# A nine-stage network on one core: scheduled layer boundaries and a first squared-relu MLP with 512-token products

## The chip, the cores and the metric

The kernel runs on one core of one Trainium2 chip. The metric is the time of one execution on the device, in microseconds (us), without the transfer of inputs and outputs to and from the host. The engines of the core are TensorE (PE, with its weight loads PEld beside it), VectorE (DVE), ScalarE (ACT), GpSimd (POOL) and SyncE (SP), which here only issues transfers. L12 in a row means line 12 of the kernel that the row was taken from.

## The reference

One sequence of 512 tokens, width 1024, runs through two networks. The first has a mixer of two attentions, a cross attention to 256 memory rows and a SwiGLU MLP of width 2816. The second has two layers: an mLSTM and an MLP, then an attention with compressed keys and values (MLA) and an MLP. All of it is float32. Every part takes a normalised stream and adds its normalised output to it; in the second network shift, scale and gate come from a conditioning vector:

```python
ada = cond @ ada_w[l] + ada_b[l]
sh1, sc1, g1, sh2, sc2, g2 = jnp.split(ada, 6, axis=-1)
h = modulate(rmsnorm(x, norm_g[l, 0]), sh1, sc1)
...
x = x + g1[:, None, :] * rmsnorm(y, norm_g[l, 1])
h = modulate(rmsnorm(x, norm_g[l, 2]), sh2, sc2)
y = sqrelu_mlp(h, mlp_w1[l], mlp_w2[l])
x = x + g2[:, None, :] * rmsnorm(y, norm_g[l, 3])
```

with `sqrelu_mlp(h, w1, w2) = jnp.square(jax.nn.relu(h @ w1)) @ w2`, inner width 4096, and `modulate(h, shift, scale) = h * (1 + scale) + shift`.

## The kernel before

**Products.** Every float32 operand is split into a high part (a rounded copy, made by ACT) and a low part (the rest, made by DVE), and a product of two operands is three matmuls: high by high, high by low, low by high (L447, L448, L449 in `prod`). Weights come by DMA from SP's queue into `raw` tiles and are split there: L307 and L308 plain, L317 and L318 with a gain in it. Activations are split by `parts` (L626 on ACT, L627 on DVE). The stream `x` stays in four tiles of 128 tokens; what a product reads is its normalised, transposed and split form `h`, an `HT` (tiles of all 512 tokens) or an `HS` (quarters of 256 tokens by four blocks of rows).

**The two squared-relu MLPs** (`relu2`, `mlp`) take their 32 hidden tiles in blocks of 6, 8, 6, 6 and 6, and add each block's down product to a sum in SBUF. Where `h` is an `HS`, which is so in both, blocks 1 to 4 go by `wino`: a pair of hidden tiles is made by seven products of 256 tokens in place of eight (L510). `split7` makes the seven weight combinations (subtractions and additions L342, L345, L361 on DVE, splits L341 on ACT), `quarters` the seven of the activations (with POOL's L482), and the results are put together from PSUM by copies on ACT and additions on DVE (L520 to L534). Block 0, and every product of an `HT`, goes by `relu_pairs`: plain products of two weight columns tiles of 128 at a time.

**Layer boundaries** (`boundary`, L634). The last block's down product of each stage yields its rows by token tile. For each of the four token tiles `a` adds the sum to `x` and takes the mean of squares (L579 on ACT, L568 and L562 on POOL), `scaled` normalises it (L598 on ACT, two halves of 512 columns), and `put` transposes it on PE (L608), modulates it where the next part wants that (two of four columns on DVE L616, two on ACT L619, into a new tile), and splits it (L626, L627), half after half. `first` is the next stage's first product, which yields at each point the token tiles it needs. All this ran in `self.ordered()`: on PE, ACT, DVE and POOL the instructions stood in the order in which the code names them. Outside, a list scheduler orders the program by priority and a model of times.

**Background.** The rows of `ada` are made by a generator that `step` calls once for each 2.0 us of PE work (`pace`, `pacb`): weights by DMA (L868, POOL's queue), multiplied on DVE (L863), summed over rows by one matmul (L881), written to `arow` in DRAM, and fetched as columns by `cols_steps` (L381 to L388: a DMA, three yields, a transpose on PE at L386).

## Time and profile before

| what | us |
|---|---|
| median of three runs | 2026.44 |
| lowest, highest | 2026.16, 2029.08 |
| profiled execution | 2028.55 |
| its span | 2026.5 |

The span is from the first to the last instruction of the profiled execution; 2.05 us lie around it. The stages follow each other in the span so: mixer 0 to 476, cross attention to 545, SwiGLU to about 833, mLSTM to about 1045, first squared-relu MLP 1075 to 1457, attention to about 1650, second squared-relu MLP from 1667 to 2019. Neighbours overlap by some microseconds, since a stage's first products run beside the boundary of the one before. PE's busy time is that of matmul instructions with modelled ends; a time in which PE waits is named by the instruction that waited and by the one whose end released it.

### The profile page before, as it was taken

What the parts mean: (1) busy time and instruction counts of PE and PEld (TensorE: products, weight loads), DVE (VectorE), ACT (ScalarE), POOL (GpSimd) and SP (SyncE); (2) the same over time, 40 slices, a digit from 0 to 9 for tenths busy, and PEclk for the clock granted to TensorE, in tenths of its full rate; (3) what the DMA queues carried; (4) which work ended last, traced back from release to release, by engine and by line L of the source; (5) the groups of instructions that cost most, each with busy time, mean ns of one, the idle gap of its engine ahead of it and who ended that gap; (6) DMA issues with size and microseconds to landing.
All of it is one profiled execution on the core that took longest, in us unless ns stands there. A gap on an engine that the chain in (4) does not pass through costs nothing. (4 is left out here: it accounts for less than half of the span.)

```text
span 2026.5 us, 29742 instructions
## 1 busy us (share of the span) xinstructions
PE 1943.2 (96%) x10738; PEld 1663.4 (82%) x10738; DVE 1373.4 (68%) x2689; ACT 1073.1 (53%) x2355; POOL 355.6 (18%) x711
## 2 busy tenths in 40 slices
PE   7999999999999999899999899998889989999997
PEld 5888988878888888678888788888687879989996
DVE  5756655856666665576866888898568747657665
ACT  6767775545353243556446464455465556545543
POOL 1331111201122211121323221222120012000000
PEclk9999999999999999999999999999999999999999
DMA  6322342523465554153442354565243212233321
GB/s 198 89 79 65 113 136 74 187 73 115 136 208 177 161 172 116 52 169 101 154 135 84 110 162 138 185 188 165 62 114 94 84 63 73 73 114 105 104 85 62
DMA packets 175251, 242.01 MB, mean 119 GB/s; under 512 B 20108, under 2 KB 117537, under 8 KB 175105
## 3 DMA queue, kind: packets, MB, share of 16 engines
q1 hardware_dynamic: 150704, 170.53, 27.2%
q0 software_dynamic: 24400, 69.60, 11.5%
q8 instruction: 84, 1.38, 0.3%
q14 instruction: 63, 0.51, 0.1%
HBM read 237.88 MB, written 2.20 MB: 118 GB/s over the span
## 5 line engine op out<-in xcount | busy, mean ns | idle before, releaser
L447 PE MATMUL ps<-s,s 128*128 128x512 f32 (+4 forms) x2276 | 863.0, 381 | 26.7 <-ACT s L626 25.1
L448 PE MATMUL ps<-s,s 128*128 128x512 f32 (+4 forms) x2276 | 851.6, 375 | 2.8 <-DVE s L627 1.9
L449 PE MATMUL ps<-s,s 128*128 128x512 f32 (+4 forms) x2276 | 849.7, 375 | 1.5 <-DVE s L627 1.4
L447 PEld LDWEIGHTS ps<-s,s 128*128 128x128 f32 (+2 forms) x2276 | 432.0, 190 | 105.9 <-ACT s L626 31.0
L449 PEld LDWEIGHTS ps<-s,s 128*128 128x128 f32 (+2 forms) x2276 | 431.2, 190 | 83.2 <-DVE s L627 5.2
L448 PEld LDWEIGHTS ps<-s,s 128*128 128x128 f32 (+2 forms) x2276 | 432.3, 190 | 79.1 <-DVE s L627 4.0
L510 PEld LDWEIGHTS ps<-s,s 128*128 128x128 f32 x2184 | 261.8, 188 | 6.7 <-DVE u L526 4.5
L510 PE MATMUL ps<-s,s 128*128 128x256 f32 x2184 | 263.7, 281 | 3.6 <-DVE u L526 3.6
L307 ACT ACTIVATE s<-raw 128x512 fp32r<-128x512 f32 x277 | 157.8, 622 | 143.2 <-PE ps L449 97.9
L308 DVE TENSOR_TENSOR s<-raw,s 128x512 fp32r<-128x512 f32 x277 | 190.3, 726 | 57.0 <-ACT s L307 55.7
L863 DVE SCALAR_TENSOR_TENSOR u<-araw,cond,u 128x512 f32<-128x512 f32 x224 | 167.3, 747 | 24.2 <-DMA araw<-in_ada_w 15.4
L317 ACT ACTIVATE s<-raw,cols_all 128x256 fp32r<-128x256 f32 (+1 forms) x305 | 143.5, 546 | 66.5 <-PE ps L449 29.8
L318 DVE SCALAR_TENSOR_TENSOR s<-raw,cols_all,s 128x256 fp32r<-128x256 f32 (+1 forms) x305 | 147.6, 538 | 39.3 <-ACT s L317 38.7
L868 POOL DMA_DIRECT2D araw<-in_ada_w x192 | 104.0, 542 | 338.0 <-DVE u L863 289.2
L627 DVE TENSOR_TENSOR s<-u,s 128x512 fp32r<-128x512 f32 x126 | 87.0, 700 | 79.4 <-ACT s L626 56.7
L626 ACT ACTIVATE s<-u 128x512 fp32r<-128x512 f32 x126 | 77.6, 625 | 63.8 <-PE ps L449 31.9
L568 POOL TENSOR_SCALAR sm<-sm,sm 128x1 f32<-128x1 f32 x34 | 10.5, 307 | 527.5 <-ACT junk L579 527.4
L341 ACT ACTIVATE s<-raw 128x512 fp32r<-128x512 f32 x104 | 62.7, 621 | 72.7 <-PE ps L449 37.6
L627 DVE TENSOR_TENSOR s<-ps,s 128x512 fp32r<-128x512 f32 (+3 forms) x100 | 59.1, 606 | 42.4 <-ACT s L626 35.0
L341 ACT ACTIVATE s<-u 128x512 fp32r<-128x512 f32 x78 | 48.7, 624 | 66.8 <-DVE u L345 36.4
L342 DVE TENSOR_TENSOR s<-raw,s 128x512 fp32r<-128x512 f32 x104 | 70.7, 683 | 15.4 <-ACT s L341 15.1
L1358 DVE TENSOR_TENSOR u<-ps,u 128x512 f32<-128x512 f32 x80 | 53.9, 685 | 34.3 <-PE ps L449 33.6
(261 smaller groups left out, 2162.9 us busy)
## 6 DMA issues: line engine op xcount, KB each, us to landing
raw<-in_mlp_w SPq DMA_DIRECT2D x128, 512.0 KB, 3.8
araw<-in_ada_w POOLq DMA_DIRECT2D x192, 256.0 KB, 3.5
raw<-in_w_gate_up SPq DMA_DIRECT2D x44, 512.0 KB, 4.1
raw<-in_w_in SPq DMA_DIRECT2D x24, 512.0 KB, 4.2
raw<-in_a_w_in SPq DMA_DIRECT2D x24, 512.0 KB, 3.8
raw<-in_w_down SPq DMA_DIRECT2D x22, 512.0 KB, 3.7
raw<-in_w_mem_kv SPq DMA_DIRECT2D x16, 512.0 KB, 3.6
araw<-in_kv_ada_w POOLq DMA_DIRECT2D x32, 256.0 KB, 4.0
```

The lines of the kernel that those rows point to most:

```text
L307: A.activation(hi[:, sl, cl], src[:, sl, cl], AF.Copy)
L308: f.tensor_tensor(out=lo[:, sl, cl], in0=src[:, sl, cl], in1=hi[:, sl, cl].bitcast(F32), op=ALU.subtract)
L317: A.activation(hi[:, i, :], src[:, i, :], AF.Copy, scale=g)
L318: V.scalar_tensor_tensor(out=lo[:, i, :], in0=src[:, i, :], scalar=g, in1=hi[:, i, :].bitcast(F32), op0=ALU.mult, op1=ALU.subtract)
L341: A.activation(hi, x, AF.Copy)
L447: self.nc.tensor.matmul(ps, lhsT=ah, rhs=bh, start=first and i == 0, stop=False)
L448: self.nc.tensor.matmul(ps, lhsT=ah, rhs=bl, start=False, stop=False)
L449: self.nc.tensor.matmul(ps, lhsT=al, rhs=bh, start=False, stop=last and i == n - 1)
L510: nc.tensor.matmul(ps, lhsT=l[:, k, :], rhs=m[:, k, :], start=first and k == e == 0, stop=k == 3 and e == 2, skip_group_check=True)
L627: self.nc.vector.tensor_tensor(out=lo, in0=x, in1=hi.bitcast(F32), op=ALU.subtract)
L863: V.scalar_tensor_tensor(out=acc, in0=raws.pop(j), scalar=vec[:, j:j + 1], in1=acc, op0=ALU.mult, op1=ALU.add)
L868: nc.gpsimd.dma_start(out=raws[j], in_=ws[:, j, :])
```

## The change

Five things change.

1. The first squared-relu MLP gets its activations as an `HT`. So `relu2` takes all its blocks by `relu_pairs`, 512 tokens at a time, and neither `wino`, `split7` nor `quarters` is called there. The second keeps its `HS`.
2. `boundary` no longer runs in `self.ordered()`; no layer boundary has a fixed order. The boundary's own steps get a higher priority (`self.hot("hb")`, an offset of 300). With `fixed=False`, which only the first squared-relu MLP's boundary has, they also stand in another place of the program: `put` of the tile two before and all `scaled` ahead of the next stage's first products.
3. `put` modulates both halves of a token tile, in place in the normalised tile, and then splits both.
4. `pace` and `pacb` go from 2.0 to 1.9, `lc` (weight tiles split ahead in an MLP's last block) from 7 to 6, and `cols_steps` yields five times between its DMA and its transpose.
5. At the start the tiles 1 to 3 of `x` are fetched two or so weight tiles earlier.

```diff
-        for _ in range(3):
+        for _ in range(5):
             yield None
...
+        todo = []
         for y, cw in ys:
...
-            hi, lo = h.blk(k, n, tt(t))
             if mod:
                 g, sh = mod
-                y = self.u2((P, n, P))
+                y = y.rearrange("p (n c) -> p n c", c=P)
...
                 ps = y
+            todo.append((k, n, ps))
+            k += n
+        for k, n, ps in todo:
+            hi, lo = h.blk(k, n, tt(t))
             self.parts(hi, lo, ps)
-            k += n
...
-        with self.ordered():
+        hot = lambda: self.hot("hb")
+        with nullcontext():
...
-                    if n == 4 and nxt and t >= 2:
+                    if n == 4 and nxt and t >= 2 and fixed:
                         self.put(*pend.pop(t - 2))
-                if nxt and t >= 1:
-                    scaled(t - 1)
-                rs[t] = a(t, ys, ss)
+                with hot():
+                    if nxt and t >= 2 and not fixed:
+                        self.put(*pend.pop(t - 2))
+                    if nxt and t >= 1:
+                        scaled(t - 1)
+                    rs[t] = a(t, ys, ss)
             if nxt:
-                i = -1
+                if not fixed:
+                    with hot():
+                        scaled(NT - 1)
                 for i, need in enumerate(first):
-                    if i == late[0]:
+                    if fixed and i == late[0]:
                         scaled(NT - 1)
-                    for n, t in ((1, NT - 2), (2, NT - 1)):
-                        if i == late[n]:
-                            self.put(*pend.pop(t))
+                    for t in sorted(pend):
+                        if t <= need if not fixed else i >= late[t - 1]:
+                            with hot():
+                                self.put(*pend.pop(t))
...
-        self.before = {2: [lambda: get(1)], 4: [lambda: get(2), lambda: get(3)], 6: [biases]}
+        self.before = {1: [lambda: get(1)], 3: [lambda: get(2), lambda: get(3)], 6: [biases]}
...
-        hn = HS(self, KD)
+        hn = HT(self, KD)
         self.out_lin(a["a_w_out_2"][0], ho, g, nxt(4, 3, hn), self.relu_pairs(hn, a["mlp_w1_2"][0], 0, BUF["fp"], True), "head")
```

Lines behind the changed ones shift by up to ten: L881 and L598 of before are L891 and L598 of after, L626 is L629, L1693 is L1703.

The order on PE just behind the boundary before the first squared-relu MLP, before: L881 sums a background row, L386 transposes columns, and the others are products; the numbers behind a name tell tiles apart.

```order
4853 L448 MATMUL ps_10803<-s_2021_10571,s_1989_10414 128x256
4854 L449 MATMUL ps_10803<-s_2021_10571,s_1989_10414 128x256
4855 L881 MATMUL ps_10855<-u_2052_10828,onesr_78 128x512
4856 L386 MATMUL ps_10911<-ident_66,u_2055_10873 128x8
4857 L447 MATMUL ps_10979<-s_1995_10449,s_2044_10785 128x512
```

The same place in the changed kernel:

```order
4875 L449 MATMUL ps_11018<-s_2062_10814,s_2097_11010 128x512
4876 L891 MATMUL ps_11103<-u_2106_11082,onesr_78 128x512
4877 L447 MATMUL ps_11018<-s_2062_10814,s_2097_11010 128x512
...
4930 L449 MATMUL ps_11134<-s_2066_10876,s_2081_10914 128x512
4931 L386 MATMUL ps_11187<-ident_66,u_2111_11125 128x8
4932 L447 MATMUL ps_11134<-s_2066_10876,s_2080_10913 128x512
```

The transpose stood directly behind the row's sum; now 54 product matmuls stand between the two.

The order on PE where the last block's down product of the first squared-relu MLP begins, before. L510 are the seven products of the last pairs, s_2453, s_2454 and s_2498 the hidden tiles: one to four in the first two, five and six in the last.

```order
5622 L447 MATMUL ps_14007<-s_2489_13903,s_2453_13669 128x512
5623 L448 MATMUL ps_14007<-s_2489_13903,s_2453_13669 128x512
5624 L510 MATMUL ps_13831<-s_2021_10571,s_2473_13795 128x256 x12
5625 L449 MATMUL ps_14007<-s_2489_13903,s_2454_13670 128x512
5626 L510 MATMUL ps_13833<-s_2064_10938,s_2474_13814 128x256 x12
5627 L447 MATMUL ps_14007<-s_2493_13942,s_2498_13975 128x512
```

The same place in the changed kernel; ps_13109 is the last hidden tile's product, s_2386 and s_2387 hold hidden tiles one to four and s_2404 five and six.

```order
6072 L449 MATMUL ps_13109<-s_2017_10495,s_2382_13015 128x512
6073 L447 MATMUL ps_13197<-s_2390_13072,s_2386_13027 128x512
...
6084 L449 MATMUL ps_13197<-s_2392_13091,s_2387_13028 128x512
6085 L447 MATMUL ps_13197<-s_2398_13146,s_2404_13177 128x512
...
6088 L447 MATMUL ps_13222<-s_2400_13165,s_2386_13027 128x512
...
6101 L448 MATMUL ps_13222<-s_2407_13190,s_2404_13177 128x512
6102 L447 MATMUL ps_13197<-s_2398_13146,s_2404_13177 128x512
```

Before, a product with the fifth hidden tile stood right behind the last of the seven products. Now the 15 rows from 6073 to 6087 and the 14 from 6088 to 6101 use hidden tiles one to five, and row 6102 is the first with the sixth.

The order on ACT at the boundary behind that MLP, before: L579 takes mean squares, of x or of a tile u of the attention, L598 normalises, L317 splits weights.

```order
1132 L579 ACTIVATE junk_14319,sm_14318<-x_11_92 128x1024
1133 L317 ACTIVATE s_2562_14261<-raw_13994,cols_2283_12462 128x384
1134 L317 ACTIVATE s_2568_14279<-raw_14003,cols_2283_12462 128x384 x2
1135 L317 ACTIVATE s_2569_14288<-raw_14264,cols_2283_12462 128x384
1136 L579 ACTIVATE junk_14371,sm_14370<-u_2589_14368 128x256
1137 L598 ACTIVATE u_2594_14377<-u_2589_14368,sm_14375 128x256
1138 L598 ACTIVATE u_2598_14389<-x_11_92,sm_14323 128x512
1139 L598 ACTIVATE u_2599_14391<-x_11_92,sm_14323 128x512
```

The same place in the changed kernel (L629 is the split of a token tile):

```order
1040 L579 ACTIVATE junk_13509,sm_13508<-x_11_92 128x1024
1041 L629 ACTIVATE s_2451_13391<-ps_13646 128x4x128
1042 L598 ACTIVATE u_2487_13515<-x_11_92,sm_13513 128x512
1043 L598 ACTIVATE u_2488_13517<-x_11_92,sm_13513 128x512
1044 L579 ACTIVATE junk_13564,sm_13563<-u_2495_13561 128x256
```

The last token tile's normalisation stood behind the weight splits and the attention's first tile; it now stands ahead of both. On POOL the DMA that fetches the bias row for that tile (L585) moved from behind the last boundary step to a place in the boundary before the MLP.

## Rows read from the trace of the kernel before

**Rows 1.** The page's first lines: the span, then for each engine its busy us, their share of the span and its instructions.

```profile
span 2026.5 us, 29742 instructions
PE 1943.2 (96%) x10738; PEld 1663.4 (82%) x10738; DVE 1373.4 (68%) x2689; ACT 1073.1 (53%) x2355; POOL 355.6 (18%) x711
```

**Rows 2.** The windows: of each stretch (us from the span's start) its length, then PE, PEld, DVE, ACT and POOL busy (and the number of their instructions), the granted clock as a share of full speed, the DMA share and GB/s. First plain products in the first network's MLP, then the whole first squared-relu MLP, then 50 us of it.

```profile
550.00:800.00 250.00, 250.00 (x1083) 202.77 (x1082) 163.94 (x289) 92.95 (x195) 49.93 (x94) 1.00 0.52 163
1075.00:1457.00 382.00, 359.92 (x2195) 319.62 (x2195) 311.20 (x519) 192.17 (x361) 87.78 (x153) 0.96 0.46 142
...
1300.00:1350.00 50.00, 46.45 (x322) 42.64 (x321) 49.10 (x87) 28.13 (x53) 11.44 (x22) 1.00 0.58 175
```

**Rows 3.** The chain that ended last, a stretch of PE in the second squared-relu MLP: start, us, engine, what, line and count of instructions that follow each other.

```profile
1950.69 25.50 PE ps L510 x216
```

**Rows 4.** The groups by line on DVE from 1130 to 1400 us, inside the first squared-relu MLP: line, engine, operation, tiles, shapes and count, busy us and mean ns of one, and the idle time before them.

```profile
L342 DVE TENSOR_TENSOR s<-raw,s 128x512 fp32r<-128x512 f32 x52 | 35.4, 681 | 4.7 <-ACT s L341 4.6
L308 DVE TENSOR_TENSOR s<-raw,s 128x512 fp32r<-128x512 f32 x41 | 26.7, 684 | 0.3
L361 DVE SCALAR_TENSOR_TENSOR u<-u,raw 128x512 f32<-128x512 f32 x13 | 8.9, 683 | 0.0
L526 DVE TENSOR_TENSOR u<-ps,u 128x256 f32<-128x256 f32 x12 | 5.0, 415 | 0.0
```

**Rows 5.** The waits of PE from 1100 to 1200 us: what waited for what, us in total, times, the longest.

```profile
PE ps L386 <- DMA u<-arow: 5.8, 2, 4.7
```

**Rows 6.** The windows, of PE alone: stretch, its length, PE busy (instructions), granted clock, DMA share, GB/s.

```profile
1120.90:1124.30 3.40, 3.36 (x9) 0.50 0.00 0
1407.60:1411.10 3.50, 3.50 (x10) 0.51 0.52 143
1421.20:1428.10 6.90, 5.48 (x12) 0.50 0.74 221
1474.30:1479.30 5.00, 4.97 (x21) 0.50 0.14 32
1544.50:1547.60 3.10, 3.06 (x12) 0.50 0.00 0
29.60:35.50 5.90, 5.90 (x18) 0.50 0.60 162
```

**Rows 7.** The waits of PE from 1250 to 1345 us.

```profile
PE ps L510 <- DVE u L526: 3.6, 3, 1.7
```

**Rows 8.** The waits of PE from 1400 to 1430 us, where the down product of the first squared-relu MLP's last block begins.

```profile
PE ps L447 <- ACT s L626: 5.0, 2, 3.3
PE ps L881 <- DVE u L627: 3.6, 1, 3.6
PE ps L449 <- DVE s L627: 1.4, 1, 1.4
```

**Rows 9.** The boundary behind that MLP: the waits of PE from 1458 to 1482 us, then the timeline from 1457 to 1476 us of ACT, of DVE and of POOL (start, us, engine, line, operation, tiles and count, in brackets the idle time before and what ended it).

```profile
PE ps L608 <- ACT u L598: 8.8, 2, 7.5
...
1471.65 0.42 ACT L579 ACTIVATE junk<-u 128x256 bf16<-128x256 f32 x1 [4.51 <-DVE u L1693]
1473.57 1.32 ACT L598 ACTIVATE u<-x,sm 128x512 f32<-128x512 f32 x2
...
1471.07 0.49 DVE L1693 TENSOR_TENSOR u<-ps,row 128x320 f32<-128x320 f32 x1 [3.21 <-DMA row<-arow]
...
1465.50 0.56 POOL L562 TENSOR_TENSOR sm<-sm,mhalf 128x1 f32<-128x1 f32 x1
1466.00 1.16 POOL L585 DMA_DIRECT2D row<-arow  x2
```

**Rows 10.** The entry of the attention: the waits of PE from 1536 to 1550 us, then a group by line on DVE from 1524 to 1548 us.

```profile
PE ps L1824 <- DVE u L1833: 4.5, 2, 2.5
...
L863 DVE SCALAR_TENSOR_TENSOR u<-araw,cond,u 128x512 f32<-128x512 f32 x6 | 4.5, 748 | 0.1
```

**Rows 11.** The start: the waits of PE from 0 to 40 us, then the timeline of ACT from 14 to 32 us.

```profile
PE ps L447 <- ACT s L626: 4.8, 2, 3.9
...
21.36 3.98 ACT L317 ACTIVATE s<-raw,cols_mix 128x8 fp32r<-128x8 f32 x16
25.84 2.43 ACT L317 ACTIVATE s<-raw,cols_mix 128x128 fp32r<-128x128 f32 x8
```

**Rows 12.** Three other boundaries: the waits of PE from 820 to 862 us (before the mLSTM), from 1040 to 1080 us (before the first squared-relu MLP) and from 1640 to 1690 us (before the second, two rows), then the groups by line on DVE and on ACT from 1660 to 1692 us.

```profile
PE ps L608 <- ACT u L598: 4.8, 3, 2.8
...
PE ps L447 <- ACT s L626: 3.5, 2, 3.1
...
PE ps L447 <- ACT s L626: 4.9, 2, 3.1
PE ps L608 <- ACT u L598: 2.8, 2, 1.6
...
L308 DVE TENSOR_TENSOR s<-raw,s 128x512 fp32r<-128x512 f32 x8 | 7.3, 958 | 3.6 <-ACT s L307 3.6
L616 DVE TENSOR_SCALAR u<-ps,cols,cols 128x128 f32<-128x128 f32 x12 | 4.3, 402 | 0.0
...
L619 ACT ACTIVATE u<-ps,cols,cols 128x128 f32<-128x128 f32 x12 | 4.8, 453 | 10.0 <-DVE u L616 8.5 <-issue 1.5
L626 ACT ACTIVATE s<-u 128x512 fp32r<-128x512 f32 x6 | 3.8, 630 | 0.2
```

More of the change, by code (lines that the diff above doesn't have):

```diff
@@ L32 @@
 ALL = slice(0, S)
-BUF = dict(s8=14, u2=15, row=2, raw=4, w0=4, w1=4, w2=4, w3=5, w4=5, w5=5, w6=5, w7=5, ps=8, pace=2.0, pacb=2.0, man=0, lag=3, lagx=3, lagm=3, half=1, quiet=1, xp=0, fp=2, r1=1.25, r1b=3.6, r1c=2.4, r2=1.6, r2b=2.6, rx=1.4, rm=0.6, pre=10, gl=3, pl=0, hb=300, hs=0, ha=0, sp=0, spq=1.3, sq=1, b1=1, b2=1, lc=7, ar=4, mb=(6, 8, 6, 6, 6), mc=(4, 3, 4, 4, 4), st2=1, pr2=8, z1=4.5, z2=5, gt=3, rv=2, gs=1, rl=3, n1=4, ex=2, em=3, vg=1, sb=(8, 8, 6), mo=4, x1=2, g0=20, st=1, y1=0, y2=1, y3=0, ph=0, pq=0, fy=1, u1=6, s32=4, sm=60)
+BUF = dict(s8=14, u2=15, row=2, raw=4, w0=4, w1=4, w2=4, w3=5, w4=5, w5=5, w6=5, w7=5, ps=8, pace=1.9, pacb=1.9, man=0, lag=3, lagx=3, lagm=3, half=1, quiet=1, xp=0, fp=2, r1=1.25, r1b=3.6, r1c=2.4, r2=1.6, r2b=2.6, rx=1.4, rm=0.6, pre=10, gl=3, pl=0, hb=300, hs=0, ha=0, sp=0, spq=1.3, sq=1, b1=1, b2=1, lc=6, ar=4, mb=(6, 8, 6, 6, 6), mc=(4, 3, 4, 4, 4), st2=1, pr2=8, z1=4.5, z2=5, gt=3, rv=2, gs=1, rl=3, n1=4, ex=2, em=3, vg=1, sb=(8, 8, 6), mo=4, x1=2, g0=20, st=1, y1=0, y2=1, y3=0, ph=0, pq=0, fy=1, u1=6, s32=4, sm=60)
 TWO_PI = 2.0 * np.pi
@@ L631, in parts, with boundary @@
                                                 op0=ALU.mult, op1=ALU.subtract)
-    def boundary(self, y_of, nxt, first, late=(1, 1, 2)):
+    def boundary(self, y_of, nxt, first, late=(1, 1, 2), fixed=True):
         V = self.nc.vector
@@ L1331, in cross, with mlp @@
         return ho
-    def mlp(self, blocks, up, w_down, g, nxt, first, ready=None, caps=None):
+    def mlp(self, blocks, up, w_down, g, nxt, first, ready=None, caps=None, fixed=True):
         nc, V = self.nc, self.nc.vector
@@ L1374, in y_of @@
                     return acc[t], ms
-                self.boundary(y_of, nxt, first)
+                self.boundary(y_of, nxt, first, fixed=fixed)
             else:
@@ L1465, in relu2 @@
         quarters = []
-        self.mlp(BUF['mb'], up, self.a["mlp_w2_2"][l], g, nxt, first, ready, BUF['mc'])
+        self.mlp(BUF['mb'], up, self.a["mlp_w2_2"][l], g, nxt, first, ready, BUF['mc'], fixed=nxt is None)
     VW = 129
```

## The prediction

> **What bounds the kernel now.** I read the page's first lines, then the windows by stage, then PE's waits in each stretch where it idled, then the timelines of what it waited for. The first lines show TensorE (PE) busy for 1943.2 of a span of 2026.5 us, VectorE (DVE) for 68% [rows 1]; so about 83 us of PE idle are all that a reordering can win, and PE's own work is the floor. The windows show that this idle time sits in a few places. From 550 to 800 us, plain products of 512 tokens with the same background work beside them, PE has no idle time: 250.00 of 250.00. In the first MLP, 1075 to 1457, it is busy for 359.92 of 382.00, and between 1300 and 1350 DVE is the full engine (49.10 of 50) while PE does 46.45 [rows 2]. So the first MLP is where PE waits for DVE, and the rest of the idle time stands at layer boundaries. After an idle stretch the granted clock is seen at 0.50 of full speed for some microseconds, that is at 1.2 GHz and not 2.4 [rows 6]; half of PE's busy time in such a stretch is lost, and I count it with the wait ahead of it.
>
> All sums are made against the profiled execution (2028.55 us, a span of 2026.5 and 2.05 around it); the median of the runs, 2026.44, lies 2.1 below it.
>
> **1. Products of 512 tokens in the first MLP.** Blocks 1 to 4 hold 26 hidden tiles, 13 pairs. A pair now takes 7 products x 4 x 3 = 84 matmuls of 256 columns; run densely 216 of them took 25.50 us, 0.118 each [rows 3], so 9.9 us. Then it takes 2 x 8 x 3 = 48 matmuls of 512 columns, at 250.00/1083 = 0.231 us [rows 2] 11.1 us. The difference of 1.16 us times 13 is **+15.1 us** of PE, all on the path, since PE is the floor. Bounds: +13 if missing records make 0.231 too long (219 in 50 us gives 0.228), +18 if a 512 column matmul costs twice a 256 column one.
>
> What goes with it: per pair 11 subtractions and additions of weights (L342, L361 and the like, 0.68 us each) become 4, and 5 combinations of PSUM halves (L526 and its like, 0.42) vanish [rows 4]: 4.8 + 2.1 = 6.9 us of DVE per pair, 90 us in 13 pairs. DVE is busy for 311.20 of 382.00 us there [rows 2], so it comes down to some 220 and is no longer full. The waits for L526 (3.6 us between 1250 and 1345 [rows 7]) have no instruction left that could make them: **-3.6**.
>
> **2. The start of the last block's down product (1400 to 1430).** The waits are 5.0 for ACT's split, 3.6 for the background row's DVE piece and 1.4 for DVE's split, 10.0 together [rows 8]; two half-clock stretches follow, with 3.50 and 5.48 of PE work, so 1.75 + 2.7 = 4.5 lost [rows 6]. Before, the last hidden tiles' relu, square and split waited for DVE's combinations, and background rows and weight splits stood between. In the new order whole products of the last pair and the part of the down product that needs no late tile stand there: the rows of PE show 12 to 15 matmuls of older tiles twice before the first that needs the newest, 29 x 0.231 = 6.7 us of cover for a chain of relu, square and split of about 2.6 us (four operations at 0.63 to 0.68, as L626 and L342 take [rows 4, 12]). I leave 1.5 us: **-13**, bounds -14.5 and -3. The faster pace (1.9 for 2.0 us of PE work per background step) also ends the background's rows 5% sooner, and in the new program they end inside the first MLP.
>
> **3. Column transposes.** PE waited 5.8 us in two L386 for a DMA that had been issued only three background steps before [rows 5]; behind it 3.36 us ran at half clock, 1.7 lost [rows 6]. Now five steps lie between, and PE's order has 54 matmuls there, 54 x 0.231 = 12.5 us, against one DMA write and one read of some microseconds each: **-7.5**, bounds -7.5 and -2.
>
> **4. No fixed order at the boundary of the first MLP to the attention.** The wait is 8.8 us in L608, one of them 7.5. The chain is read from three engines: POOL's L562 for the last token tile ends at 1466.06, ACT's normalisation L598 could start then, but stands in the written order behind ACT's L579 of the attention's own tile, which waits for DVE's L1693, and that for a bias row whose DMA POOL issued at 1466.00, after its last boundary step. So L598 started at 1473.57, 7.5 us late [rows 9]. In the new order L598 comes directly behind L579 of x, and POOL issues the row a whole MLP earlier. 4.97 us of half clock behind it cost 2.5 [rows 6]. 11.3 at most; the chain itself stays, with PE's 48 + 14 + 9 matmuls of other token tiles as its cover: **-8**, bounds -11 and 0.
>
> **5. Attention entry (1536 to 1550).** PE waits 4.5 us for DVE's L1833, and six background L863 of 0.75 us stand among DVE's work there [rows 10]; 3.06 us at half clock cost 1.5 [rows 6]. With the background ended earlier, 4.5 us of DVE leave this stretch: **-4**, bounds -6 and 0.
>
> **6. Start.** The third token tile's split waited on ACT behind 16 and then 8 small weight splits, 3.98 and 2.43 us; PE waited 4.8 in all, then ran 5.90 us at half clock [rows 11, 6]. The new order has 13 in place of 24, 11 x 0.27 = 2.9 us less, but weight loads now stand behind two x tiles on SP's queue: **-3**, bounds -8 and +3.
>
> **7. Other boundaries.** The waits are 4.8 for L608 before the mLSTM, 3.5 for L626's split before the first MLP, 7.7 (4.9 and 2.8) before the second [rows 12]. Modulating both halves first lets DVE's L616 of the second half run beside ACT's L619 of the first: per half L616 two times 0.40, L619 two times 0.45, then L626 0.63 [rows 12]; the second half's split comes some 1.5 us sooner, the first's 0.8 later. Since PE can start on either half's columns only in order, the two nearly cancel. In the new order eight weight splits (L307) still stand before the second tile's L619. I take 0 for the last two (bounds -4 and +4 each), and -2 for the first, where the scaling stands earlier (bounds -5 and +4).
>
> **8. Waits that no row shows.** What is no longer ordered by hand can stall in new places. No row sizes this; I choose half a microsecond at each of six boundaries, **+3**, bounds 0 and (rival A) +28.
>
> Sum: 15.1 - 3.6 - 13 - 7.5 - 8 - 4 - 3 - 2 + 3 = **-23 us**; 2005.5 on the profiled execution, 2003.4 on the median. I forecast **2004 us**.
>
> **Rivals.**
> *A, slower: weight splits ahead of the boundary.* With no fixed order, eight of the next stage's weight splits run on DVE before a boundary's step: 8 x 0.96 = 7.7 us [rows 12], and 1.7 of half clock behind it as in rows 6. At three boundaries this is +28, more than the 23 won: +5, 2031.6. It decides from the third boundary on. For it: these splits stand before the second tile's modulation in both orders, and DVE was slow there (L308 at 0.96 us [rows 12] against 0.68 in the first MLP [rows 4]). Against: at the place of step 4 the new order has only four small ones ahead of the last tile's mean square and none between that and L598. Chance 0.07.
> *B, the waits come back.* The stops of steps 1, 2 and 5 were made by the background and the weight loads, not by DVE's load: -3.6 and -4 become 0, and -13 becomes -3. The sum is then -5.4, 2021. For it: two of the three waits of rows 8 follow a background piece. Against: from 550 to 800 the same background ran beside plain products without any wait. Chance 0.15, a little under half of it within 0.2%.
> *C, more.* With DVE free in the first MLP nothing waits there, the remainders of steps 2, 4 and 5 go too (1.5 + 3.3 + 2), no new wait comes (3), and half of the 11 us at the last two boundaries goes with a little of its clock: -23 - 16, 1987. Against: eight L307 still stand before the second tile there. Chance 0.13.
> *D, PE is the only bound.* The idle time is there for other reasons and merely moves, so the products' +15.1 stand alone: 2041.5. Against: the DMA wait of rows 5 is made by no busy engine. Chance 0.02. [...]
>
> **How the numbers follow.** The forecast has 0.63, with a range of its own from 1994 to 2014; A 0.07, B 0.15, C 0.13, D 0.02. Runs of this kernel tell 0.2%, about 4 us, from no change. Faster: 0.63 + 0.13 + 0.08 of B = 0.84; same 0.07; slower 0.09. The range of 8 in 10 reaches down into C and up through B: 1986 to 2025, with about 0.08 left out below and 0.11 above.
>
> **What would show it.** Right: no L526 and no wait above 1 us in the first MLP; L386 without a wait; PE's 50 us windows there at 49 or more; the wait for L598 behind the first MLP under 2 us; DVE busy in that MLP near 220 us; the MLP some 15 us of matmuls longer but 10 to 15 us shorter in all. Wrong: a granted clock of 0.5 at places where it was full before, PE waiting for ACT's L307 or L626 at a boundary for over 5 us, or the last block's down product still late.

## The result and the profile after

The changed kernel takes 1996.41 us (median of 4 runs, 1995.13 to 2000.39), against 2027.67 for the kernel before on the same chip: ratio 0.9849, 95% interval 0.9832 to 0.9866, 31 us less. Its profiled execution took 1995.13, with a span of 1993.3.

The page's first lines, as in [rows 1]:

```profile
span 1993.3 us, 28466 instructions
PE 1941.7 (97%) x10222; PEld 1645.7 (83%) x10222; DVE 1276.1 (64%) x2517; ACT 1037.3 (52%) x2282; POOL 351.5 (18%) x703
```

PE is busy for about as long as before, though it now does the dearer products. Its idle time (span less busy) fell from 83.3 to 51.6 us. Laid out by stage, each from the end of the last update of `x` (L648 before, L651 after) to that of the next:

| stage | length before | after | PE idle before | after |
|---|---|---|---|---|
| start and mixer | 343.3 | 342.2 | 14.8 | 18.3 |
| cross attention | 126.7 | 131.3 | 3.0 | 5.8 |
| SwiGLU | 385.2 | 383.3 | 6.3 | 0.0 |
| mLSTM | 226.6 | 226.8 | 5.8 | 11.2 |
| first squared-relu MLP | 382.1 | 371.5 | 22.6 | 0.0 |
| attention | 210.2 | 188.5 | 18.9 | 8.6 |
| second MLP to the end | 352.4 | 349.7 | 11.9 | 7.8 |

By these updates the first two stages end earlier than the list of stages ahead of the change has them: in before the mixer at 343.3 us and the cross attention at 470.0.

The windows of the last two rows of before and of the last three of after (columns as in [rows 2]):

```profile
1463.90:1674.10 210.20, 191.26 (x1069) 167.09 (x1069) 140.09 (x349) 120.06 (x283) 28.33 (x59) 0.96 0.30 88
1674.10:2026.50 352.40, 340.48 (x2125) 305.07 (x2123) 228.32 (x380) 171.77 (x325) 17.23 (x18) 0.99 0.28 88
```

```profile
1083.60:1455.10 371.50, 371.50 (x1728) 307.05 (x1727) 211.06 (x332) 160.32 (x293) 66.41 (x124) 1.00 0.43 136
1455.10:1643.60 188.50, 179.91 (x1017) 158.34 (x1017) 120.84 (x322) 113.11 (x274) 18.07 (x34) 0.98 0.26 79
1643.60:1993.30 349.70, 341.95 (x2154) 308.13 (x2153) 218.25 (x377) 169.43 (x321) 14.97 (x18) 0.99 0.27 85
```

In the first MLP PE has no idle time at all, and DVE is at 211 of 371 us, not at 311 of 382 [rows 2]. The lengths of the rows are not gains by themselves, since the free order lets products of the next stage start before the last update of `x`: the attention's stretch has 52 matmuls fewer than before (1017 for 1069), and the second MLP's has 29 more. Of the attention's 21.7 us 10.3 are idle time; what was won is read better from the idle time. The waits of PE of 1 us and more in the whole span of after (us in total, times, the longest):

```profile
PE ps L447 <- ACT s L629: 28.5, 9, 6.1
PE ps L386 <- DMA u<-in_g_mix_pre: 5.6, 1, 5.6
PE ps L891 <- DVE u L630: 2.8, 1, 2.8
PE ps L609 <- DVE u L1623: 2.2, 1, 2.2
PE ps L449 <- DVE s L630: 2.0, 1, 2.0
PE ps L1834 <- DVE u L1843: 1.0, 2, 0.6
```

Gone are L510's waits, those of the column transposes in the middle, and every wait for L598 [rows 5, 7, 9]. Two thirds of what is left in this list is one kind: L447 waits for ACT's split of a token tile (28.5 us). Two of these waits are new; in before PE waited 0.5 us for this split at either place. This is ACT's timeline at the boundary behind the mixer in after, and PE's waits there (325 to 345 us):

```profile
331.47 1.06 ACT L579 ACTIVATE junk<-x 128x1024 bf16<-128x1024 f32 x1 [0.54 <-DVE x L651]
332.44 0.19 ACT L579 ACTIVATION_READ_ACCUMULATOR junk<-x 128x1 f32 x1
332.53 6.48 ACT L317 ACTIVATE s<-raw,cols_all 128x256 fp32r<-128x256 f32 x16
338.91 0.57 ACT L579 ACTIVATE junk<-ps 128x512 bf16<-128x512 f32 x1
339.39 0.19 ACT L579 ACTIVATION_READ_ACCUMULATOR junk<-ps 128x1 f32 x1
339.48 1.06 ACT L629 ACTIVATE s<-ps 128x512 fp32r<-128x512 f32 x2
```

```profile
PE ps L447 <- ACT s L629: 4.9, 1, 4.9
```

With no fixed order, sixteen weight splits, 6.48 us of ACT, stand in front of the next token tile's split L629, and PE waits 4.9 us. The same is seen behind the cross attention (fifteen splits, 6.08 us; a wait of 5.0) and behind the mLSTM (eight, 4.26 us; 6.1, where it was 3.1 [rows 12]).

### The profile page after: what moved, and what is told of

Read it like the earlier page. It is cut to its first block, busy times and chain, and to the rows that moved or that the text cites. A ratio compares the mean times of both kernels' runs of the same rounds, so it can differ in the third digit from the quotient of the medians.

```text
span 1993.3 us, 28466 instructions
## 1 busy us (share of the span) xinstructions
PE 1941.7 (97%) x10222; PEld 1645.7 (83%) x10222; DVE 1276.1 (64%) x2517; ACT 1037.3 (52%) x2282; POOL 351.5 (18%) x703
## 4 chain that ended last, share of the span: by engine, by line
PE 90%; ACT 4%; DVE 4%; issue 1%; DMA 0%; POOL 0%; SPq 0%; DVEq 0%; POOLq 0%; ACTq 0%
PE ps L447 25%; PE ps L448 24%; PE ps L449 24%; PE ps L510 6%; PE ps L1033 1%; PE ps L609 1%; PE ps L1823 1%; ACT s L317 1%; PE ps L1852 1%; PE ps L1004 1%; PE ps L1583 1%; DVE s L318 1%; PE ps L1017 1%; PE ps L1320 1%; ACT junk L579 1%
## 5 line engine op out<-in xcount | busy, mean ns | idle before, releaser
L447 PE MATMUL ps<-s,s 128*128 128x512 f32 (+3 forms) x2468 | 940.2, 383 | 28.5 <-ACT s L629 28.5
L448 PE MATMUL ps<-s,s 128*128 128x512 f32 (+3 forms) x2468 | 928.3, 377 | 0.1
L449 PE MATMUL ps<-s,s 128*128 128x512 f32 (+3 forms) x2468 | 924.4, 377 | 2.0 <-DVE s L630 2.0
L447 PEld LDWEIGHTS ps<-s,s 128*128 128x128 f32 (+1 forms) x2468 | 467.2, 190 | 114.6 <-ACT s L629 31.5
L449 PEld LDWEIGHTS ps<-s,s 128*128 128x128 f32 (+1 forms) x2468 | 466.3, 189 | 91.3 <-DVE s L630 2.5
L448 PEld LDWEIGHTS ps<-s,s 128*128 128x128 f32 (+1 forms) x2468 | 467.3, 189 | 83.7 <-DVE s L630 1.0
L307 ACT ACTIVATE s<-raw 128x512 fp32r<-128x512 f32 x329 | 186.3, 623 | 177.3 <-PE ps L449 130.7
L308 DVE TENSOR_TENSOR s<-raw,s 128x512 fp32r<-128x512 f32 x329 | 213.9, 688 | 87.8 <-ACT s L307 85.9
L317 ACT ACTIVATE s<-raw,cols_all 128x256 fp32r<-128x256 f32 (+1 forms) x305 | 142.7, 544 | 59.5 <-PE ps L449 25.2
L630 DVE TENSOR_TENSOR s<-u,s 128x512 fp32r<-128x512 f32 x118 | 80.1, 689 | 115.1 <-ACT s L629 92.6
L510 PEld LDWEIGHTS ps<-s,s 128*128 128x128 f32 x1092 | 130.2, 188 | 1.0
L510 PE MATMUL ps<-s,s 128*128 128x256 f32 x1092 | 130.5, 280 | 0.0
L629 ACT ACTIVATE s<-u 128x512 fp32r<-128x512 f32 x118 | 72.2, 627 | 53.6 <-PE ps L449 27.0
L630 DVE TENSOR_TENSOR s<-ps,s 128x512 fp32r<-128x512 f32 (+3 forms) x100 | 59.5, 606 | 36.9 <-ACT s L629 35.8
L1465 ACT ACTIVATE u<-ps 128x512 f32<-128x512 f32 x38 | 22.6, 596 | 114.9 <-PE ps L449 111.0
L629 ACT ACTIVATE s<-ps 128x512 fp32r<-128x512 f32 (+3 forms) x100 | 51.2, 526 | 23.5 <-PE ps L609 10.2
L318 DVE SCALAR_TENSOR_TENSOR s<-raw,cols_mix,s 128x128 fp32r<-128x128 f32 (+2 forms) x152 | 52.4, 401 | 11.0 <-ACT s L317 10.6
```

The lines of the kernel that those rows point to most:

```text
L307: A.activation(hi[:, sl, cl], src[:, sl, cl], AF.Copy)
L308: f.tensor_tensor(out=lo[:, sl, cl], in0=src[:, sl, cl], in1=hi[:, sl, cl].bitcast(F32), op=ALU.subtract)
L317: A.activation(hi[:, i, :], src[:, i, :], AF.Copy, scale=g)
L318: V.scalar_tensor_tensor(out=lo[:, i, :], in0=src[:, i, :], scalar=g, in1=hi[:, i, :].bitcast(F32), op0=ALU.mult, op1=ALU.subtract)
L447: self.nc.tensor.matmul(ps, lhsT=ah, rhs=bh, start=first and i == 0, stop=False)
L448: self.nc.tensor.matmul(ps, lhsT=ah, rhs=bl, start=False, stop=False)
```

## The experiments

Each run is timed beside the kernel before; the ratio is to that. The changed kernel has 0.9849 (0.9832 to 0.9866).

| run | what | median us | ratio | 95% interval |
|---|---|---|---|---|
| hs | after, part 1 undone | 2006.77 | 0.9886 | 0.9865 to 0.9907 |
| ord | after, part 2 undone | 2007.53 | 0.9897 | 0.9882 to 0.9912 |
| mix | after, order fixed at four boundaries | 1985.63 | 0.9784 | 0.9768 to 0.9801 |
| bg | after, steps of part 4 undone | 1997.61 | 0.9845 | 0.9831 to 0.9860 |
| only_ht | before and part 1 | 2030.08 | 1.0007 | 0.9997 to 1.0017 |
| only_free | before and part 2 | 2006.35 | 0.9893 | 0.9878 to 0.9908 |
| put | after, part 3 undone | 1999.80 | 0.9863 | 0.9848 to 0.9877 |
| xload | after, part 5 undone | 2001.43 | 0.9869 | 0.9855 to 0.9884 |
| ht_pace | before, part 1, pace 1.9 | 2018.78 | 0.9950 | 0.9935 to 0.9964 |
| bg_only | before, steps of part 4 | 2038.76 | 1.0048 | 1.0033 to 1.0063 |
| mix_pace | mix with pace 2.0 up to the mLSTM | 1987.22 | 0.9790 | 0.9773 to 0.9806 |
| hs_dve | hs, quarters' additions on DVE | 1996.85 | 0.9847 | 0.9830 to 0.9863 |

**hs: the quarters and seven products back.**

```diff
-        hn = HT(self, KD)
+        hn = HS(self, KD)
```

> The changed kernel, but the first squared-relu MLP again takes its activations in quarters of 256 tokens, so seven products in place of eight with their weight combinations on DVE (part 1 undone, all else as changed). Theory 'DVE was the limit there': PE has 15 us less work, but the waits for DVE come back (3.6 for the combinations, up to 14.5 at the last block's start with its half clock, some 6 us of waits too short to be listed), so about 2005 us, 5 to 10 slower than the changed kernel, with DVE busy 90 us longer. Rival 'the order did it all': the free order has removed the waits at the last block by itself, the products are pure cost, so 15 us faster than the changed kernel, about 1981.

It took 2006.77, as the first theory said. The waits for the combinations came back too (L510, 6.8 us in all, the longest 4.4 for ACT's L530), those at the last block's start did not, and two others made the greater part. PE's two longest waits from 1100 to 1200 us, then DVE's and POOL's timelines:

```profile
PE ps L891 <- DVE u L630: 4.7, 1, 4.7
PE ps L386 <- DMA u<-arow: 3.7, 1, 3.7
```

```profile
1127.47 10.62 DVE L345 TENSOR_TENSOR u<-raw,raw 128x512 f32<-128x512 f32 x1
1138.12 0.69 DVE L630 TENSOR_TENSOR u<-u,u 64x512 fp32r<-64x512 f32 x1
1138.83 0.69 DVE L345 TENSOR_TENSOR raw<-raw 128x512 f32<-128x512 f32 x1
```

```profile
1127.58 9.95 POOL L482 TENSOR_TENSOR u<-s 128x512 f32<-128x512 f32 x8
```

One DVE subtraction takes 10.62 us, the next of the same line 0.69. Beside it stand the eight additions of `quarters` on POOL, back to back. What stood behind it on DVE, L630 for the background row, was late, and so PE's L891 and, through the row's DMA, L386.

**hs_dve: the same, with those additions on DVE.**

```diff
-                G.tensor_tensor(out=x, in0=hi[:, k].bitcast(F32), in1=lo[:, k].bitcast(F32), op=ALU.add)
+                V.tensor_tensor(out=x, in0=hi[:, k].bitcast(F32), in1=lo[:, k].bitcast(F32), op=ALU.add)
```

> The run with quarters of 256 tokens again (part 1 undone), but the eight additions per MLP that rebuild the quarters' sums run on DVE and not on POOL. In that run one DVE subtraction took 10.62 us, not 0.69, while eight additions stood back to back on POOL, and PE then waited 4.7 us for a background row's sum and 3.7 us for a column transpose. Theory 'POOL's additions held DVE up': eight more DVE operations of about 0.7 us, no DVE operation above 2 us, both waits under 1.5 us, 1996 to 2003 us. Rival 'DVE is merely full there': the same work in another place, the waits stay, 2004 to 2010 us.

It took 1996.85, the theory's time and that of the changed kernel; the four runs, 1992.48 to 1998.49, all lie below those of hs, 2000.16 to 2008.47. DVE's timeline at that place and PE's waits from 1100 to 1200 us:

```profile
1121.85 4.91 DVE L482 TENSOR_TENSOR u<-s 128x512 f32<-128x512 f32 x8
1126.67 0.68 DVE L345 TENSOR_TENSOR u<-raw,raw 128x512 f32<-128x512 f32 x1
```

```profile
PE ps L510 <- ACT s L341: 3.0, 2, 2.2
PE ps L510 <- DVE u L526: 0.5, 1, 0.5
```

Eight additions cost DVE 4.9 us, the long operation is gone, and L891 and L386 do not wait. So with the free order the two forms of the first MLP are worth the same, once POOL's additions are out of the way: its stretch is 367.4 us here and 371.5 in after, with 359.1 and 371.5 of PE busy. The dearer products and the waits and half clock that they end nearly cancel. (The edit moves the second MLP's additions as well; its stretch takes 348.2 us here and 348.4 in hs, so the gain does not lie there.) What the additions on DVE are worth in the kernel before, with its fixed order, no run shows.

**only_ht: the 512-token products alone.** (The diff of hs, the other way round, on the kernel before.)

> The kernel before with nothing but the 512-token products in the first squared-relu MLP (part 1 alone). In the run with quarters the transposes of L386 waited again although five steps lay in front of them; so the theory now is that this wait, too, comes from a DVE that is behind with the background rows. Theory 'DVE': with part 1 alone L386 no longer waits (three steps as before), the start of the last block waits less, 2008 to 2018 us with 15 us more PE work. Rival 'steps and order': the wait of 5.8 us for L386 and the wait at the last block stay, 2024 to 2042.

The time is the rival's, 2030.08, no difference from before; but the waits went as the theory said. The windows of the first MLP, the attention and the second MLP:

```profile
1082.10:1451.50 369.40, 366.32 (x1687) 301.08 (x1687) 207.91 (x326) 158.50 (x287) 63.79 (x123) 1.00 0.43 136
1451.50:1661.20 209.70, 191.02 (x1060) 166.50 (x1059) 144.48 (x358) 119.73 (x282) 34.50 (x70) 0.96 0.35 100
1661.20:2026.30 365.10, 345.72 (x2137) 309.29 (x2136) 233.33 (x393) 172.45 (x327) 20.13 (x29) 0.98 0.28 89
```

The first MLP wins what was expected, 12.7 us (369.4 for 382.1), with L386 and the last block's start no longer waiting. The second MLP loses the same 12.7 (365.1 for 352.4). The groups of the background's sum in only_ht and, for comparison, in after (count, first and last start), and PE's waits from 1664 to 1700 us in only_ht:

```profile
L881 PE MATMUL ps<-u,onesr x30: 307/392/794, 390.1 to 1693.9; 128*128 128x512 f32 x28, 128*128 128x320 f32 x1, 128*128 128x384 f32 x1
```

```profile
L891 PE MATMUL ps<-u,onesr x30: 308/395/796, 384.0 to 1341.6; 128*128 128x512 f32 x28, 128*128 128x320 f32 x1, 128*128 128x384 f32 x1
```

```profile
PE ps L881 <- DVE u L627: 5.0, 1, 5.0
PE ps L447 <- ACT s L626: 2.8, 1, 2.8
PE ps L448 <- DVE s L627: 1.5, 2, 1.2
```

The last row's sum stands at 1694 us, in the second MLP, where the kernel before had none (its last is at 1633), and PE waits for it there. The code says why: a plain product lowers the count by 0.65 for every three matmuls, so 2.0 is used up after four of them (2.6) and 1.9 after three (1.95); a seven-product step lowers it by 0.34, which takes six either way. Plain products at 2.0 slow the background, and 1.9 makes it a third faster, not 5%. In the SwiGLU, from 550 to 800 us, 7 sums run before and 10 after.

**ht_pace: part 1 and the pace.**

```diff
-        hn = HS(self, KD)
+        hn = HT(self, KD)
...
-pace=2.0, pacb=2.0
+pace=1.9, pacb=1.9
```

> The kernel before with the 512-token products in the first squared-relu MLP and 1.9 in place of 2.0 us of PE work for a background step (part 1 and the pace of part 4; fixed order and three steps at the column transposes kept). Part 1 alone won 12.6 us in the first MLP and lost 12.7 in the second, where the last two background rows' sums now stood (1677 and 1694 us, a wait of 5.0 us in front of one). A plain product takes steps of 0.65, so a background step comes after four of them at 2.0 and after three at 1.9. Theory 'part 1 only pays if the background keeps up': all rows end before 1400 us, the second MLP takes 352 us again, the attention's entry does not wait for L1833, 2005 to 2016 us. Rival 'the fixed order eats the gain': 2022 to 2032.

2018.78, 11 less than only_ht, just above the range. The second MLP takes 352.0 again, the attention 200.4, and the last sum stands at 1312 us. Against that the mLSTM, which gets rows earlier, takes 237.9 for 226.6, with a wait of 6.6 us for a row's sum (L881).

**bg_only: the pace and five steps alone, on the kernel before.** (The diffs of bg, the other way round.)

> The kernel before with nothing but the two numbers of part 4: 1.9 us for a background step and five steps between a column DMA and its transpose. Theory 'the steps of seven-product work are 0.34, six of them either way, but in the rest of the network the background runs a third faster': the rows end before 1480 us, the attention's entry does not wait, L386 may wait while DVE is full; 2014 to 2024 us. Rival 'five per cent of pace do nothing': 2024 to 2030.

Both ranges were wrong: 2038.76, slower than before. The rows do end early (the last sum stands at 1369 us), and the attention takes 200.4 us for 210.2. Against that the mLSTM takes 239.4 for 226.6, with the wait of 6.6 us for L881 that ht_pace has too, and the first MLP 388.3 for 382.1. PE's longest waits from 1100 to 1400 us, and what DVE and POOL did before the longest of them:

```profile
PE ps L881 <- DVE u L627: 8.4, 2, 6.9
PE ps L386 <- DMA u<-arow: 6.1, 1, 6.1
PE ps L510 <- ACT u L530: 4.3, 1, 4.3
```

```profile
1134.35 10.62 DVE L345 TENSOR_TENSOR u<-raw,raw 128x512 f32<-128x512 f32 x1
1134.44 9.97 POOL L482 TENSOR_TENSOR u<-s 128x512 f32<-128x512 f32 x8
```

It is the event of hs: the row's split L627 comes directly behind that subtraction, at 1144.99, and PE's L881 at 1145.83, after 6.9 us. L386 fetches this row; it waits 6.1 us though five steps lie in front of it. So the longest wait came from POOL's additions, and the second from the DVE work that had piled up behind them; what the faster background costs beside the seven products without them, no run shows. The greater loss, 12.8 us, lies in the mLSTM, which has none of these products.

**bg: the steps of part 4 undone.**

```diff
-        for _ in range(5):
+        for _ in range(3):
             yield None
...
-pace=1.9, pacb=1.9
+pace=2.0, pacb=2.0
```

> The changed kernel with three steps between a column DMA and its transpose again, and a background step for each 2.0 us of PE work (the two numbers of part 4 but lc undone). Theory 'a transpose issued too early stops PE': L386 waits 3 to 7 us again and some half clock follows, 1999 to 2005 us. Rival 'the free order puts matmuls in front of it anyway': L386 does not wait, 1994 to 1998.

1997.61, not told apart from the changed kernel: the rival. L386 has no wait in the middle of the kernel with three steps. PE's waits at the attention's entry (1500 to 1545 us) in bg:

```profile
PE ps L1834 <- DVE u L1843: 4.7, 2, 2.7
PE ps L1823 <- DVE s L630: 0.3, 1, 0.3
```

The slower background is back at the attention's entry (4.7 us, 1.0 in after; the attention takes 195.4 us for 188.5), and the mLSTM is 6 us shorter (220.6), without after's waits for L891 and L1623. The two cancel. The third number of part 4, `lc`, was not run by itself.

**ord: the fixed order at all boundaries.**

```diff
-        hot = lambda: self.hot("hb")
-        with nullcontext():
+        hot = nullcontext
+        with self.ordered():
...
-        self.mlp(BUF['mb'], up, self.a["mlp_w2_2"][l], g, nxt, first, ready, BUF['mc'], fixed=nxt is None)
+        self.mlp(BUF['mb'], up, self.a["mlp_w2_2"][l], g, nxt, first, ready, BUF['mc'])
```

> The changed kernel with every layer boundary in the fixed order again (part 2 undone; also no raised priority and the old places of the steps at the boundary behind the first MLP). The trace of the changed kernel has new waits of 4.9, 5.0 and 6.1 us at the boundaries behind the mixer, the cross attention and the mLSTM, and has lost 6.3 behind the SwiGLU and about 9 behind the first MLP. Theory 'the free order gives at two boundaries and takes at three': the two nearly cancel, 1994 to 2004 us, with L598 late by about 7 us behind the first MLP again and no wait over 2 us at the first two boundaries. Rival 'the free order is a main gain': 2012 or more.

2007.53, between the two. The waits behind the mixer and the cross attention are gone, and 2.8 us for L598 behind the SwiGLU are back. Behind the first MLP PE waits 5.0 us, but for a weight split of the attention (L317), not for L598. L598 is nearly as late as in [rows 9] (ACT starts it at 1463.48, 6.5 us after POOL's L562 has ended), but PE has other products then and does not wait for it. PE's idle time is 55.7 us in all, for 51.6 in after.

**only_free: the free order alone, on the kernel before.** (Part 2 of the diff.)

> The kernel before with nothing but the free order at the boundaries (part 2 alone, with its raised priority and the moved steps behind the first MLP). Theory 'free order gives at the MLPs' boundaries and takes at the attentions'': 2014 to 2022 us, L598 not late behind the first MLP, no wait behind the SwiGLU, new waits of about 5 us behind the mixer and the cross attention, and the waits of the first MLP's inside (L386, L510) still there. Rival 'the order only helps once DVE is free': 2024 or more.

2006.35, better than the first theory said; the mechanism was as it said, but for L386, which does not wait here. PE's idle time falls by 9.6 us in the first MLP, 6.3 in the SwiGLU, 4.7 in the attention and 4.4 in the second MLP, and grows by 3.8 in the mixer and 2.7 in the cross attention, each with a new wait of 4.9. (The attention's stretch is 13.7 us shorter, but with 59 matmuls fewer.) PE's waits from 1395 to 1475 us:

```profile
PE ps L888 <- DVE u L627: 3.5, 1, 3.5
PE ps L447 <- ACT s L626: 2.9, 1, 2.9
PE ps L608 <- ACT u L598: 1.8, 1, 1.8
PE ps L449 <- DVE s L627: 1.8, 1, 1.8
```

The wait of 7.5 us for L598 [rows 9] is gone, that for the row's sum (L888 here) has stayed. This part alone makes two thirds of the gain, 22 of 31 us. Taken out of the changed kernel (ord) it is worth 11: the parts overlap.

**mix: fixed order where an attention or the mLSTM ends, free order at the MLPs' ends.**

```diff
-        hot = lambda: self.hot("hb")
-        with nullcontext():
+        hot = nullcontext if order else lambda: self.hot("hb")
+        with self.ordered() if order else nullcontext():
...
-        self.boundary(y_of, nxt, first, late)
+        self.boundary(y_of, nxt, first, late, order=True)
```

> The changed kernel with the fixed order at the four boundaries behind an attention or mLSTM (those that out_lin calls), and free order at the MLPs' boundaries. Theory 'weight splits in front of the boundary's steps make the new waits': the 4.9, 5.0 and 6.1 us go, with 2 to 3 us of half clock behind each, about 1980 to 1988 us. Rival 'these boundaries wait for their own chain and a wait only changes its place': 1993 to 2000.

1985.63, faster than both kernels (ratio to before 0.9784, interval 0.9768 to 0.9801). ACT's timeline behind the mixer, and PE's waits from 325 to 345 us:

```profile
335.14 0.90 ACT L317 ACTIVATE s<-raw,cols_all 128x256 fp32r<-128x256 f32 x2
335.94 1.06 ACT L629 ACTIVATE s<-ps 128x512 fp32r<-128x512 f32 x2
336.90 0.90 ACT L317 ACTIVATE s<-raw,cols_all 128x256 fp32r<-128x256 f32 x2
```

```profile
PE ps L447 <- ACT s L629: 0.5, 1, 0.5
PE ps L609 <- ACT u L598: 0.5, 1, 0.5
PE ps L448 <- DVE s L630: 0.3, 1, 0.3
```

Two weight splits stand where sixteen stood. Behind the mLSTM 4.1 of the 6.1 us stay. PE's idle time in the stretches of the mixer, the cross attention and the mLSTM is 4.1, 2.9 and 1.4 us less than in after. Order and raised priority change together in ord, mix and only_free, so the two are not told apart.

**mix_pace: 2.0 up to the mLSTM.** (`pace=2.0, pacb=1.9` in mix.)

> The version with the fixed order at the attentions' and the mLSTM's boundaries and free order at the MLPs', and 2.0 in place of 1.9 up to the mLSTM, 1.9 behind it. Its profile had waits of 2.8 us for a background row's sum and 2.2 us (L1623) inside the mLSTM, and 5.4 us lost to half clock there, none of which the run with 2.0 everywhere has. Theory 'the faster background costs in the mLSTM': 1977 to 1983 us. Rival 'what it saves there it loses in the first MLP and the attention, which get those rows': 1983 to 1990.

1987.22: the rival. The mLSTM takes 222.5 us for 231.6 in mix, the attention 198.7 for 188.6.

**put and xload: parts 3 and 5 undone.** (The old `put`; `{2: ..., 4: ..., 6: ...}` for the places of the `x` tiles.)

> The changed kernel with the old put: each half modulated into a tile of its own and split before the next half (part 3 undone). Theory 'the two nearly cancel': 1993 to 1999 us. Rival 'the earlier second half counts': the waits for ACT's split grow by 1 to 2 us at the three modulated boundaries, 1999 to 2004.

> The changed kernel with the tiles of x fetched at the old places of SP's queue (part 5 undone). Theory 'the start is bound by ACT and the transfers as before': within 2 us of the changed kernel, 1994 to 1998. Rival 'the earlier x tiles removed the small splits from ahead of the third tile's split': half a microsecond more of waiting and a longer half-clock stretch at 25 to 36 us, 1998 to 2002.

1999.80 and 2001.43, each at the rival's end, but their intervals overlap that of the changed kernel, so a gain is not shown for either part, nor excluded. In put the waits for L626 come to 31.0 us, 28.5 for L629 in after. In xload PE waits 3.9 us for the third tile's split, 3.3 in after; of the 5.4 us by which that profile is longer, 3.1 lie in the mLSTM, where the clock fell (below).

## Why the prediction was right, and where it was not

The forecast was 2004 us, 22 to 24 less; 31 were measured, inside the range of 1986 to 2025. That the sum came out well is in part luck: terms were wrong in both directions.

**Step 1, products.** The price was right. Counting PE's busy time in the first MLP's stretch less half of what ran at the half clock, after has 370.2 us and hs_dve 355.2: 15 us for the 15.1 forecast. Counted so over the whole kernel, which moved products cannot disturb, it is 13.5, and 13.3 from before to only_ht, near the lower bound of 13. What it buys was only partly right. With the fixed order it ended the waits forecast (369.4 for 382.1 in only_ht), as the expected relief of DVE (208 us busy in only_ht for 311). But under the free order most of the waits that part 1 ends have a cause that the prediction left out: POOL's additions, which held DVE up. With them on DVE the old products do as well there (hs_dve). In the kernel before no DVE instruction took more than 1.81 us, so how far POOL made its waits is not shown.

**Step 2, the last block's start.** All 10 us of waits and the clock behind them are gone, without the remainder of 1.5. Part 1 is not needed for it beside the others: in hs, where the rows end earlier, the last block does not wait either. In only_free, with neither part 1 nor the faster pace, the row's sum still waits 3.5 there.

**Step 3, column transposes.** The -7.5 came, but not by the five steps: three steps wait for nothing in bg, only_ht and only_free, and five wait 3.7 and 6.1 us in hs and bg_only. The transpose waits when the row's DMA is issued late, and in hs and bg_only that is when DVE is behind after the long subtraction. In only_free DVE is as full as before (315.02 of 377.50 us), but the row's DMA leaves at 1111.83, before POOL's additions begin at 1114.19. The sentence "Now five steps lie between" named the wrong cause.

**Step 4, free order behind the first MLP.** Right: L598 is no longer late, in only_free as in after; 2.8 us of other waits (L447, L449) stay for the 8.8, near the 3 left over. But in ord, with the fixed order back, L598 is 6.5 us late and PE does not wait for it; so its lateness alone does not make the wait.

**Step 5, attention entry.** Right in size and in what decides it: 1.0 us after, and 4.7 again in bg, where the background is slower. "5% sooner" was wrong: a third, by the counting of the steps.

**Steps 6 and 7.** The start won 2.4 us for the 3 forecast (the first token tile's update of `x` ends at 322.5 us before and 320.1 after), but not by a shorter wait: PE's waits in the first 100 us come to 12.4 us in both, while the granted clock of the first 40 us is 0.91 before and 0.96 after. The new wait behind the mixer takes 1.3 of it back. Behind the SwiGLU all 6.3 us of idle time went, not 2. At the two boundaries priced at 0, behind the mLSTM the wait grew from 3.1 to 6.1, and before the second MLP it fell from 7.7 to 4.9.

**Step 8 and rival A.** This is the term that was mis-sized: +3 for new waits. The mechanism of rival A, weight splits in front of a boundary's step, happened behind the mixer, the cross attention and the mLSTM, with up to 6.48 us of ACT where 7.7 of DVE had been named; mix shows that it costs about 11 us in all (1996.41 to 1985.63). So the term should have been near 11, an estimate from these two times. It did not decide, since the free order gave more elsewhere.

**What no step had.** Idle time fell by 31.7 us, and PE's busy time by 1.5 although the products added 13 to 15. Of that difference the half clock is 7 (half of PE's busy time in all stretches like those of [rows 6] is 19.7 us before and 12.4 after). The other 7 to 9 us went from busy time in which PE ran at full clock. Most of it came with the free order: only_free, with the same 10738 matmuls as before, has 5.7 us less of it. Waits shorter than a matmul's overlap are not listed as idle, and I take them to be these, but no run shows that by itself. Idle time and half clock together fell by 39.0 us, and the forecast's terms for waits, clock and new waits add up to 38.1; so the 8 us by which the forecast fell short are about this unlisted part.

So rival B was wrong in its reason for steps 1 and 2, whose waits ended with DVE's load in only_ht, and right for step 5, which the background decides; and its picture (what is won inside the first MLP comes back later) is what only_ht did, through the background's pace. C named the first MLP rightly (no idle time at all), and not the boundaries. D fell with the first MLP's idle time.

## What to carry to other kernels

A free schedule and a fixed order are better chosen boundary by boundary: on the engine that PE waits for, read what stands between the last needed input and the needed instruction, and fix the order where bulk work slips in. Relief for a full engine pays only if what paces the rest keeps up, so look where a background's last pieces land after the change. And before an engine is called full, look for single instructions far above their usual time.

## What the runs showed of the hardware

A DVE subtraction with two inputs in SBUF took 10.62 us while eight POOL additions of two SBUF inputs ran back to back (9.95 us in hs, 9.97 in bg_only), and 0.69 otherwise; with the additions on DVE (hs_dve) no DVE instruction took more than 1.52. In both runs it ended 0.56 us behind POOL's last addition. So, within 0.01 us, did DVE's splits that began in the middle of the eight: L627 with 8.61 us in only_free and 4.71 in only_ht, L630 with 6.37 in bg. In the kernel before the two engines took turns in place of this, at some 1.5 and 1.7 us an instruction:

```profile
1098.22 5.83 DVE L308 TENSOR_TENSOR s<-raw,s 128x512 fp32r<-128x512 f32 x4
1098.38 5.11 POOL L482 TENSOR_TENSOR u<-s 128x512 f32<-128x512 f32 x3 [1.56 <-DVE s L627]
```

What decides between the two forms is not shown. The Trainium skill ("SBUF — State Buffer", section "Who interferes with whom") says that a DVE instruction with two SBUF inputs contends with a GpSimd instruction that reads SBUF, and that the order of issue decides who blocks. The trace agrees that they contend. On the order it does not bear the page out: in hs and bg_only the DVE instruction is recorded 0.1 us ahead of POOL's first addition, and yet it was held, through eight POOL instructions and not one.

The clock after a wait is not the same each time. The row's sum in the mLSTM waited 2.8 us in after and in xload alike; these are the windows of PE of the next 10 us, after first:

```profile
890.50:900.50 10.00, 7.88 (x34) 1.00 0.31 92
```

```profile
892.00:902.00 10.00, 7.86 (x28) 0.83 0.24 70
```

In after PE kept its full clock and did 34 instructions, in xload it fell to 1.2 GHz for some 3.4 us and did 28. xload has one more such drop in the mLSTM, at 1044 us, where after has none. So the 3.1 us between the two profiles there need no cause in the edit that is compared.
